# A two-layer decoder trunk on one core: forget-gate sums by matrix products, layer 1's residual gate later in the weight stream, and more pieces open to two engines

## The chip, the cores and the metric

One core of a Trainium2 chip runs the whole kernel in one launch. The metric is the device time of the execution in microseconds (us). The engines are named as the profile names them: PE (TensorE), PEld (its weight loads), DVE (VectorE), ACT (ScalarE), POOL (GpSimd) and SP (the queue that issues the DMAs, SPq in the rows).

## The reference

The input is x with 256 rows and 1,024 columns, in f32. Each of the two layers does the same frame around a different mixer:

```
shift, scale, gate = split(silu(c) @ ada_w[layer] + ada_b[layer], 3)
h = rmsnorm(x, pre_g[layer]) * (1 + scale) + shift
y = mixer(h)                      # even: SSD + block attention; odd: forgetting attention + S5
x = x + gate * rmsnorm(y, post_g[layer])
```

Layer 0's mixer projects h, runs a causal convolution, an SSD recurrence (16 heads, chunks of 128 rows, decay matrices `exp(segsum(dt * a))`) and, at 256 rows, plain causal attention with 16 heads. Its SSD output is multiplied by silu(z) and RMS-normalised over 1,024 columns. Layer 1's mixer runs attention with 24 heads whose scores carry a forget gate, and an S5 state-space branch with 2,048 complex states:

```
F = cumsum(log_sigmoid(f_raw + fgate_b))            # per head, over the 256 rows
s = q @ k.T / 8 + F[query] - F[key];  s = -inf where key > query;  p = softmax(s)
```

F[query] is the same for a whole row of s and cancels in the softmax, so a kernel has to add only F[key].

## The kernel before

All weights pass through the core once, as a stream of units of 128x2,048 f32 (1 MB) that `stream_order` (L42) lays out and that SP loads into three `raw` buffers. A unit of a projection is taken in two halves of 128x1,024. ACT rounds a half to f32r (`whi`), and DVE or POOL subtracts to get the rest (`wlo`); PE then makes three products (high by high, high by low, low by high). There are four `whi` and four `wlo` buffers. Units of kind "mod" and "gate" are not multiplied on PE: DVE reduces a "mod" unit against the condition vector (`modulate`, L822, which makes one column of scale and one of shift), and sums a "gate" unit row by row into `acc` (`ada_piece`, L794: one TENSOR_SCALAR and three SCALAR_TENSOR_TENSOR of 128x512 for the first of two units, four of the latter for the second). `ada_done` (L807) turns `acc` into the product of gate and post-norm weights, `gpt`.

No order of instructions is written by hand. The program records all operations, each for an engine; `Plan.schedule` (L501) orders them by a list scheduler with costs and due times and searches over due times with a fixed seed; `issue` then writes each engine's instructions in the order found. That is why nearly all rows carry line L534. An operation recorded by `either2` (L674) may go to DVE or POOL, as the search decides; one recorded with `G.` goes to POOL, one with `V.` to DVE. A stream order, a buffer count or a cost that changes gives another order everywhere.

The stages follow the stream. Layer 0: the convolution's units and the first "mod" units; z, v and qk units, beside which the SSD is done in four groups of four heads (`ssd`, L1382); then out units. In `ssd` POOL multiplies the rounded and the remaining part of the decay rates (`ahi`, `alo`) by a triangular mask (`keep`) into four `r2` tiles of 128x512 for a group, PE sums them along the rows, ACT takes the exponential. POOL also multiplies the SSD's output by silu(z) (zs) and adds up the squares (ssum). Layer 1: v, u, a small projection for the forget gate, zd, zc, v, then twelve qk units, each followed by the attention of a pair of heads; eight S5 pairs are placed between units by `S5_AT`, "glu" follows the ninth qk unit, and out units end the kernel. Layer 1's four "gate" units lie in the stream behind the last four qk units.

Before, F goes to DRAM once (`fd`), and for each pair of heads `fox_add` (L1584) loads its rows back, spread over 128 partitions, by four DMAs into an `A` buffer; POOL adds the causal mask to it. In `attention` (L1051) PE makes the scores of both heads in two `st` banks of PSUM, DVE adds the prepared tile and takes the row's extreme value (CUSTOM_DVE_ANT_0 `b<-st,A`, for 128 and 256 columns, each with a read of its accumulator), ACT takes the exponentials, PE transposes, and so on. `st` has three banks, and S5 pairs use two of them for as long as DVE works on them in place.

Of the kernel before, what the change touches and what calls it, by code (L numbers as in the profile page):

```python
# [41 lines left out]
def stream_order():  # L42
# [21 lines left out]
    for i in range(12):  # L64
        s.append(("in", 1, "qk", i))
        if i == 8:
            s.append(("glu",))
        if i >= 8:
            s.append(gate1.pop(0))
    s += [("out", 1, i) for i in OUT1_ORDER]  # L70
    return s
# [545 lines left out]
def trunk(ctx, tc, par, s5par, x, w, dtw, fw, postg, gateb, out):  # L617
# [189 lines left out]
    def ada_done(l, c):  # L807
        acc = accs.pop((l, c))
        pb = bank("st")
        gb, pg = tmp("b", [P, 512]), tmp("b", [P, 512])  # L810
        n0 = 512 * c
        S.dma_start(gb, gateb[l:l + 1, n0:n0 + 512].to_broadcast([P, 512]))
        S.dma_start(pg, postg[l:l + 1, n0:n0 + 512].to_broadcast([P, 512]))
        parts = tmp("r2", [P, 512]), tmp("r2", [P, 512])
        split(acc, *parts)
        with plan.together():
            for n, t in enumerate(parts):
                T.matmul(pb, onesr, t, start=(n == 0), stop=(n == 1))
        V.tensor_add(gb, pb, gb)
        G.tensor_mul(gpt[:, n0:n0 + 512], gb, pg)  # L820

    def modulate(l, k, halves):  # L822

        md = tmp("s", [P, 2])
        for n, r in enumerate(halves):
            V.tensor_tensor_reduce(out=r, in0=r, in1=condb, scale=1.0, scalar=0.0, op0=ALU.mult, op1=ALU.add,
                                   accum_out=md[:, n:n + 1])
        c = 16 * l + 2 * k
        V.scalar_tensor_tensor(acol[:, l, k:k + 1], md[:, 0:1], adab1[:, c:c + 1], pc("preg", 8 * l + k, 8 * l + k + 1),
                               op0=ALU.add, op1=ALU.mult)  # L830
        V.tensor_add(bcol[:, l, k:k + 1], md[:, 1:2], pc("adab", c + 1, c + 2))
# [218 lines left out]

    def attention(pair, qk, v, addt, y):  # L1051

        sbs = [bank("st"), bank("st")]
        with plan.together(0.72):
            for b in range(2):
                for j in range(2):
                    h = slice(64 * j, 64 * j + 64)
                    T.matmul(sbs[j][:, BLK[b][0]], qk[h, 0, 128 * b:128 * b + 128], qk[h, 1, 0:128 * b + 128],
                             start=(b == 0), stop=(b == 1), skip_group_check=True)
        pTs = []  # L1060
        for j in range(2):
            p, mn, ad = tmp("b", [P, 384]), tmp("s", [P, 4]), addt(j)
            for c, b in BLK:
                V.tensor_tensor_reduce(out=p[:, c], in0=sbs[j][:, c], in1=ad[:, c], scale=-0.125,
                                       scalar=3.0e38, op0=ALU.add, op1=ALU.min, accum_out=mn[:, b:b + 1])
# [26 lines left out]

    def qkdone(i, vt, addt, y):
        def done(pb):
            qk = tmp("qk", [P, 2, SEQ])
            A.activation(qk, pb, AF.Copy)
            attention(i, qk, vt, addt, y)
        return done
# [276 lines left out]
    def x_decayed(q):  # L1375
        c = slice(512 * q, 512 * q + 512)
        G.tensor_mul(v3(xdt[2][:, c]), v3(xdt[0][:, c]), dtd[:, 8 * q:8 * q + 8, None].to_broadcast([P, 8, 64]))

# [3 lines left out]
    def ssd(hg):  # L1382
        ms, pv = [], {}
        for c in range(2):
            for s, src in (("h", ahi), ("l", alo)):
                t = tmp("r2", [P, 4, P])
                G.tensor_tensor(out=t, in0=src.bitcast(F32)[:, c, 4 * hg:4 * hg + 4, None].to_broadcast([P, 4, P]),
                                in1=keep[:, None, :].to_broadcast([P, 4, P]), op=ALU.mult)
                pv[c, s] = t
# [19 lines left out]
        for pr in range(2):  # L1409
# [3 lines left out]
                                   op0=ALU.mult, op1=ALU.add)  # L1413
            G.tensor_mul(zs(pair), ya, zs(pair))
            if pair == 0:
                A.activation(ssum, zs(pair), AF.Square)
            else:
                sq = tmp("a", [P, SEQ])
                A.activation(sq, zs(pair), AF.Square)
                G.tensor_add(ssum, ssum, sq)  # L1420

# [31 lines left out]

    am2 = amask.rearrange("p b k -> p (b k)")
    for i in range(8):
        proj_cm(qkdone(i, vt, lambda j: am2, zs(8 + i)))
        if i == 0:
# [56 lines left out]
    V.tensor_add(fl, fl, fo[:, 0:16, None].to_broadcast([24, 16, 16]))  # L1514
    fd = scratch([24, SEQ], "fd")
    S.dma_start(fd, flf)

# [65 lines left out]

    def fox_add(i):  # L1584
        fb = tmp("A", [P, 2, 3, P])
        for j in range(2):
            src = fd[2 * i + j:2 * i + j + 1, :]
            S.dma_start(fb[:, j, 0:1, :], src[:, 0:128].to_broadcast([P, 128]))
            S.dma_start(fb[:, j, 1:3, :], src.to_broadcast([P, 256]))
        G.tensor_add(fb, fb, amask[:, None, :, :].to_broadcast([P, 2, 3, P]))  # L1590
        return fb.rearrange("p j b k -> p j (b k)")

    def glu():
# [20 lines left out]
    for i in range(12):  # L1614
        fb = fox_add(i)
        proj_cm(qkdone(i, vt1, lambda j, fb=fb: fb[:, j, :], zc(i)))
        s5_at(14 - NV + i)
# [8 lines left out]
    with tc.manual_schedule():  # L1626
# [11 lines left out]

NA = 12

# [109 lines left out]
```

## Time and profile before

| | us |
|---|---|
| runs of the kernel | 572.38, 577.53, 578.82 (median 577.53) |
| the profiled execution | 581.22 |
| its span, from first to last instruction | 579.4 |

The profiled execution had a mean granted TensorE clock of 0.949 of full speed. Its span is what all rows refer to: times are from the span's start. The 1.8 us between span and execution lie around the instructions.

### The profile page before, as it was taken

How to read it: one execution, taken by the hardware profiler on the slowest of the kernel's cores; microseconds unless marked ns; L12 is line 12 of the kernel's file. 1: busy time of each engine (PE TensorE's matmuls, PEld its weight loads, DVE VectorE, ACT ScalarE, POOL GpSimd, SP SyncE). 2: the span in 40 equal slices, each digit the busy share in tenths (PEclk: the TensorE clock that was granted, in tenths of full speed). 3: DMA queues.
4: the chain of work that ended last, by engine and by line, in shares of the span. 5: the costliest groups of instructions: out<-in, count | busy, mean ns of one | idle time of the engine just before them, and what ended most of it. 6: DMA issues, size and time to landing. Idle time of an engine off the chain costs nothing.

```text
span 579.4 us, 10569 instructions
## 1 busy us (share of the span) xinstructions
PE 529.4 (91%) x3948; PEld 471.7 (81%) x3948; DVE 495.1 (85%) x1084; ACT 367.5 (63%) x759; POOL 121.1 (21%) x107
## 2 busy tenths in 40 slices
PE   7899969899999999896999999999989829999995
PEld 5799969789998897684999997899969617887784
DVE  7998999889989989877669989799998798788764
ACT  5546966564768776356565467367667757789641
POOL 3000315739331000001000222011313434300000
PEclk9999979899999999998799999799989858999998
DMA  8999256376323466993234274054254546635602
GB/s 311 410 408 342 74 181 250 122 258 229 145 95 141 188 245 261 345 353 133 74 111 181 93 283 146 1 218 147 92 206 137 155 157 208 221 125 212 240 24 73
DMA packets 25575, 110.02 MB, mean 190 GB/s; under 512 B 2844, under 2 KB 9652, under 8 KB 15284
## 3 DMA queue, kind: packets, MB, share of 16 engines
q1 hardware_dynamic: 25524, 109.35, 51.6%
q8 instruction: 31, 0.51, 0.3%
q14 instruction: 20, 0.16, 0.1%
HBM read 108.26 MB, written 1.07 MB: 189 GB/s over the span
## 4 chain that ended last, share of the span: by engine, by line
PE 64%; DVE 20%; ACT 6%; DMA 5%; issue 3%; SPq 0%; POOL 0%; POOLq 0%; DVEq 0%; ACTq 0%
PE mm L534 50%; PE st L534 9%; PE y L534 5%; DVE wlo L534 5%; DMA raw<-in_w_dram 4%; DVE b L534 4%; ACT b L534 2%; ACT whi L534 2%; DVE D L534 2%; DVE tb L534 2%; DVE a L534 2%; DVE st L534 1%; DMA A<-in_w_dram 1%; DVE acc L534 1%; DVE raw L534 1%
## 5 line engine op out<-in xcount | busy, mean ns | idle before, releaser
L534 ACT ACTIVATE whi<-raw 128x1024 fp32r<-128x1024 f32 x124 | 128.6, 1053 | 72.9 <-PE mm L534 48.5
L534 DVE TENSOR_TENSOR wlo<-raw,whi 128x1024 fp32r<-128x1024 f32 x112 | 142.1, 1281 | 18.7 <-ACT whi L534 18.1
L534 PE MATMUL mm<-hhi,wlo 128*128 128x256 f32 x656 | 95.8, 289 | 3.9 <-DVE wlo L534 3.9
L534 PE MATMUL mm<-hhi,whi 128*128 128x256 f32 x664 | 95.5, 285 | 2.6 <-ACT whi L534 2.6
L534 PE MATMUL mm<-hlo,whi 128*128 128x256 f32 x664 | 94.5, 283 | 0.0
L534 PEld LDWEIGHTS mm<-hhi,wlo 128*128 128x128 f32 x656 | 85.7, 194 | 8.3 <-DVE wlo L534 4.7
L534 PEld LDWEIGHTS mm<-hhi,whi 128*128 128x128 f32 x664 | 85.6, 191 | 5.5 <-ACT whi L534 3.0
L534 PEld LDWEIGHTS mm<-hlo,whi 128*128 128x128 f32 x664 | 84.7, 190 | 2.5 <-issue 2.4
L534 ACT ACTIVATE b<-b,s 128x256 f32<-128x256 f32 (+1 forms) x160 | 65.9, 445 | 22.4 <-DVE s L534 21.8
L534 PE MATMUL mm<-whi,r 128*128 128x512 f32 x240 | 68.7, 395 | 1.3 <-ACT whi L534 1.3
L534 PEld LDWEIGHTS mm<-whi,r 128*128 128x128 f32 x240 | 44.2, 188 | 11.7 <-ACT whi L534 1.7
L534 POOL TENSOR_TENSOR wlo<-raw,whi 128x1024 fp32r<-128x1024 f32 x12 | 30.3, 2532 | 104.7 <-ACT whi L534 104.7
L534 ACT ACTIVATE b<-tb,s5r 128x256 f32<-128x256 f32 (+3 forms) x128 | 42.2, 385 | 14.4 <-DVE tb L534 13.5
L534 DVE CUSTOM_DVE_ANT_0 raw<-raw,condb 128x1024 f32<-128x1024 f32 x32 | 38.3, 1216 | 1.5 <-DMA raw<-in_w_dram 1.5
L534 PE MATMUL mm<-wlo,r 128*128 128x512 f32 x120 | 38.9, 395 | 0.7 <-DVE wlo L534 0.6
L534 DVE TENSOR_TENSOR tb<-b 128x16 f32<-128x16 f32 (+3 forms) x124 | 30.1, 282 | 7.5 <-ACT b L534 7.0
L534 POOL TENSOR_TENSOR A<-A,amask 128x768 f32<-128x768 f32 x12 | 22.4, 1870 | 54.1 <-DMA A<-fd 47.2
L534 POOL TENSOR_TENSOR s<-s,nhalf 128x1 f32<-128x1 f32 (+1 forms) x9 | 6.0, 675 | 117.8 <-DVE s L534 108.1
L534 PE MATMUL st<-ident,b 128*128 128x128 f32 x128 | 20.6, 284 | 9.5 <-DVE s L534 5.4
L534 PEld LDWEIGHTS mm<-wlo,r 128*128 128x128 f32 x120 | 22.1, 188 | 6.3 <-DVE wlo L534 1.6
L534 PE MATMUL st<-qk 64*128 64x128 f32 (+1 forms) x160 | 21.2, 373 | 5.8 <-DVE b L534 5.8
L534 PEld LDWEIGHTS st<-ident,b 128*128 128x128 f32 x128 | 14.8, 143 | 14.1 <-ACT b L534 12.7
(219 smaller groups left out, 938.1 us busy)
## 6 DMA issues: line engine op xcount, KB each, us to landing
raw<-in_w_dram SPq DMA_DIRECT2D x80, 1024.0 KB, 4.9
raw<-in_w_dram SPq DMA_DIRECT2D x16, 512.0 KB, 10.4
A<-in_w_dram SPq DMA_DIRECT2D x14, 512.0 KB, 10.3
A<-fd SPq DMA_DIRECT2D x24, 128.0 KB, 4.2
A<-fd SPq DMA_DIRECT2D x24, 64.0 KB, 4.7
xres<-in_x_dram SPq DMA_DIRECT2D x2, 512.0 KB, 5.1
b<-in_gateb_dram SPq DMA_DIRECT2D x4, 256.0 KB, 6.0
b<-in_postg_dram SPq DMA_DIRECT2D x4, 256.0 KB, 6.9
```

The source lines that it names most:

```text
L534: getattr(self.engines[e], method)(*[at(v) for v in a], **{n: at(v) for n, v in k.items()})
```

## The change

- Forget gate: `fd`, `fox_add`, its 49 DMAs and 12 POOL additions go. F is kept in SBUF as a rounded part and a rest (`fr`, 2 x 24 rows, the same again in the upper 64 partitions), made by three ACT copies and a DVE subtraction. For each pair of heads PE makes four products of f32r operands ahead of the score products, in the same PSUM banks: a column of `pickf`, repeated 128 times, picks the head's two rows and adds them to all rows of s. DVE then adds the plain mask `amask`, as in layer 0.
- Layer 1's four "gate" units move in the stream from behind qk units 8 to 11 to behind the first four out units.
- `either2` takes the place of `G.` for the decay rows (`r2`), the decayed x, the z products, the sums of squares and `gpt`.
- In layer 1, `modulate` keeps its sums in a tile of 8 x 2 columns and adds bias and scale for four at a time (three operations) where it did two for each.
- `NA` falls from 12 to 11 buffers of 128x1,024, `b` rises from 7 to 8 buffers of 128x512, and `S5_AT` moves pairs 3 to 8 one unit earlier.

```diff
@@ stream_order
         if i == 8:
             s.append(("glu",))
-        if i >= 8:
+    for i in OUT1_ORDER:
+        s.append(("out", 1, i))
+        if gate1:
             s.append(gate1.pop(0))
-    s += [("out", 1, i) for i in OUT1_ORDER]
@@ ada_done, modulate
-        G.tensor_mul(gpt[:, n0:n0 + 512], gb, pg)
+        either2("tensor_mul", gpt[:, n0:n0 + 512], gb, pg)
...
-        md = tmp("s", [P, 2])
+        md = tmp("s", [P, 2]) if l == 0 else md1[:, k, :]
...
+        if l == 1:
+            if k % 4 == 3:
+                ks = slice(k - 3, k + 1)
+                V.tensor_add(bcol[:, 1, ks], md1[:, ks, 1], ab4[:, 1, ks, 1])
+                V.tensor_add(md1[:, ks, 0], md1[:, ks, 0], ab1[:, 1, ks, 0])
+                V.tensor_mul(acol[:, 1, ks], md1[:, ks, 0], pre2[:, 1, ks])
+            return
@@ attention
+        if gates:
+            pick, rows = gates
+            with plan.together(0.3):
+                for b in range(2):
+                    for j in range(2):
+                        h, n = slice(64 * j, 64 * j + 64), 2 * pair + j
+                        T.matmul(sbs[j][:, BLK[b][0]], pick[h, n:n + 1].to_broadcast([64, P]), rows[h, 0:128 * b + 128],
+                                 start=(b == 0), stop=False, skip_group_check=True)
...
-            p, mn, ad = tmp("b", [P, 384]), tmp("s", [P, 4]), addt(j)
+            p, mn = tmp("b", [P, 384]), tmp("s", [P, 4])
             for c, b in BLK:
-                V.tensor_tensor_reduce(out=p[:, c], in0=sbs[j][:, c], in1=ad[:, c], scale=-0.125,
+                V.tensor_tensor_reduce(out=p[:, c], in0=sbs[j][:, c], in1=am2[:, c], scale=-0.125,
@@ x_decayed, ssd
-        G.tensor_mul(v3(xdt[2][:, c]), v3(xdt[0][:, c]), dtd[:, 8 * q:8 * q + 8, None].to_broadcast([P, 8, 64]))
+        either2("tensor_mul", v3(xdt[2][:, c]), v3(xdt[0][:, c]), dtd[:, 8 * q:8 * q + 8, None].to_broadcast([P, 8, 64]))
...
-                G.tensor_tensor(out=t, in0=src.bitcast(F32)[:, c, 4 * hg:4 * hg + 4, None].to_broadcast([P, 4, P]),
-                                in1=keep[:, None, :].to_broadcast([P, 4, P]), op=ALU.mult)
+                either2("tensor_mul", t, src.bitcast(F32)[:, c, 4 * hg:4 * hg + 4, None].to_broadcast([P, 4, P]),
+                        keep[:, None, :].to_broadcast([P, 4, P]))
...
-            G.tensor_mul(zs(pair), ya, zs(pair))
+            either2("tensor_mul", zs(pair), ya, zs(pair))
...
-                G.tensor_add(ssum, ssum, sq)
+                either2("tensor_add", ssum, ssum, sq)
@@ forget gate
-    fd = scratch([24, SEQ], "fd")
-    S.dma_start(fd, flf)
+    G.memset(fr.bitcast(F32), 0.0)
+    i4 = ident.rearrange("p (g n) -> p g n", n=32)
+    V.tensor_add(pickf[0:64], i4[0:64, 0], i4[0:64, 1])
+    V.tensor_add(pickf[64:P], i4[64:P, 2], i4[64:P, 3])
+    A.activation(fr[0:24], flf, AF.Copy)
+    sub2(fr[32:56], flf, fr[0:24].bitcast(F32))
+    for n in range(2):
+        A.activation(fr[64 + 32 * n:88 + 32 * n], fr[32 * n:32 * n + 24].bitcast(F32), AF.Copy)
...
-    def fox_add(i):
-        fb = tmp("A", [P, 2, 3, P])
-        for j in range(2):
-            src = fd[2 * i + j:2 * i + j + 1, :]
-            S.dma_start(fb[:, j, 0:1, :], src[:, 0:128].to_broadcast([P, 128]))
-            S.dma_start(fb[:, j, 1:3, :], src.to_broadcast([P, 256]))
-        G.tensor_add(fb, fb, amask[:, None, :, :].to_broadcast([P, 2, 3, P]))
-        return fb.rearrange("p j b k -> p j (b k)")
@@ constants
-NA = 12
+NA = 11
-S5_AT = (0, 1, 3, 5, 7, 9, 11, 13)
+S5_AT = (0, 1, 2, 4, 6, 8, 10, 12)
-        "D": (2048, 1), "a": (256, 5), "b": (512, 7),
+        "D": (2048, 1), "a": (256, 5), "b": (512, 8),
```

How the scheduler's order comes out is seen in the two programs. Their instructions were counted by kind. PE has 48 more (24 of 128 and 24 of 256 columns, `st<-fr,pickf`). POOL has 17 subtractions `wlo<-raw,whi` of 128x1,024 where it had 12, and 4 of the 16 decay products where it had all; DVE has the other 12, 4 of the 8 z products, 5 of the 7 sums of squares and 2 of the 4 `gpt` products, and 107 subtractions `wlo<-raw,whi` where it had 112. SP has 131 DMA instructions where it had 180.

The first place is POOL and DVE in layer 0, where the SSD's first two groups are prepared (`r` are the `r2` tiles, `dtd` and `cbt` are decay factors). POOL before:

```order
L534 TENSOR_TENSOR alo<-dtk,ahi 128x32
L534 TENSOR_TENSOR r_75<-ahi,keep 128x512
L534 TENSOR_TENSOR r_78<-ahi,keep 128x512
L534 TENSOR_TENSOR r_79<-alo,keep 128x512
L534 TENSOR_TENSOR r_76<-alo,keep 128x512
L534 TENSOR_TENSOR A_113<-A_2_488,dtd 128x512
L534 TENSOR_TENSOR r_77<-alo,keep 128x512
```

and DVE now, where the same products stand between subtractions for the next weights:

```order
L535 TENSOR_TENSOR wlo_72<-raw_63,whi_66 128x1024
L535 TENSOR_TENSOR r_75<-alo,keep 128x512
L535 TENSOR_TENSOR r_76<-alo,keep 128x512
L535 TENSOR_TENSOR wlo_71<-raw_65,whi_68 128x1024
L535 TENSOR_TENSOR r_75<-ahi,keep 128x512
L535 TENSOR_SCALAR acc_74<-raw_64,cond 128x512
```

So the products have moved from a queue of their own into the one that also makes `wlo`.

The second place is DVE in layer 1, at the last S5 pair (`s5mag` is its scan, `s_` with 128x1 the accumulator of a row's extreme value, `A_2_3343` the tile of `fox_add`). Before:

```order
L534 SCALAR_TENSOR_TENSOR b_94<-s5mag,st_128 128x256 x2
L534 RECIPROCAL s_96<-s_96 128x2
L534 SCALAR_TENSOR_TENSOR acc_74<-raw_65,cond,acc_74 128x512
L534 ISA b_92,s_100<-st_127,A_2_3343 128x128
L534 ISA s_100 128x1
L534 ISA b_92,s_100<-st_127,A_2_3343 128x256
L534 ISA s_100 128x1
L534 TENSOR_TENSOR b_93<-b_94,tb_109 128x512
L534 RECIPROCAL s_100<-s_100 128x2
L534 SCALAR_TENSOR_TENSOR acc_74<-raw_65,cond,acc_74 128x512
```

and now:

```order
L535 SCALAR_TENSOR_TENSOR b_90<-s5mag,st_128 128x256 x2
L535 ISA b_96,s_103<-st_126,amask 128x256
L535 ISA s_103 128x1
L535 RECIPROCAL s_103<-s_103 128x2
L535 TENSOR_TENSOR b_93<-b_90,tb_110 128x512
L535 ISA b_94,s_101<-st_128,amask 128x128
L535 ISA s_101 128x1
L535 ISA b_94,s_101<-st_128,amask 128x256
```

The sums into `acc` are gone from here. Of the 24 wide row-extreme instructions of layer 1 (128x256), 17 followed the last S5 scan before, and 19 do now. The first sum into `acc` of layer 1 stood behind 6 of the 24; now it stands behind 14.

The third place is PE where a pair of heads begins (`qk` are its queries and keys), now:

```order
L535 MATMUL mm_125<-hhi,wlo_71 128x256 x8
L535 MATMUL st_126<-fr,pickf 128x128
L535 MATMUL st_127<-fr,pickf 128x128
L535 MATMUL st_126<-fr,pickf 128x256
L535 MATMUL st_127<-fr,pickf 128x256
L535 MATMUL st_126<-qk_82 128x128
L535 MATMUL st_127<-qk_82 128x128
L535 MATMUL st_126<-qk_82 128x256
L535 MATMUL st_127<-qk_82 128x256
L535 MATMUL mm_124<-hhi,whi_67 128x256 x8
```

The gate products stand right ahead of the score products in ten of the twelve pairs; in two, other rows of PE lie between.

## Rows read from the trace of the kernel before

**Rows 1.** The page's head: the span, the engines' busy time, share of the span and instructions, and the chain that ended last by engine.

```profile
span 579.4 us, 10569 instructions
PE 529.4 (91%) x3948; PEld 471.7 (81%) x3948; DVE 495.1 (85%) x1084; ACT 367.5 (63%) x759; POOL 121.1 (21%) x107
...
PE 64%; DVE 20%; ACT 6%; DMA 5%; issue 3%; SPq 0%; POOL 0%; POOLq 0%; DVEq 0%; ACTq 0%
```

**Rows 2.** Busy time by stretch of the span. The columns are the stretch, its length, busy us (and instructions) of PE, PEld, DVE, ACT and POOL, the granted clock, the DMA engines' mean busy share, and GB/s.

```profile
72.00:148.00 76.00, 67.58 (x543) 63.94 (x542) 69.77 (x99) 47.12 (x65) 41.07 (x34) 0.93 0.55 202
148.00:264.00 116.00, 113.85 (x793) 97.60 (x792) 99.72 (x271) 76.52 (x166) 9.45 (x18) 1.00 0.60 226
264.00:284.00 20.00, 14.44 (x74) 12.62 (x73) 17.37 (x45) 13.55 (x37) 2.22 (x4) 0.74 0.30 106
357.00:371.00 14.00, 11.84 (x69) 10.48 (x68) 12.16 (x28) 5.79 (x12) 2.45 (x1) 0.76 0.15 64
457.00:481.00 24.00, 11.59 (x60) 7.42 (x64) 21.66 (x55) 13.88 (x37) 9.13 (x7) 0.54 0.46 152
481.00:510.00 29.00, 28.42 (x246) 23.89 (x239) 21.96 (x63) 22.07 (x64) 11.40 (x6) 0.97 0.64 215
```

**Rows 3.** Who waited for whom from 450 to 510 us: us in total, times, the longest.

```profile
PE st L534 <- DVE b L534: 5.8, 1, 5.8
PE st L534 <- DVE s L534: 5.4, 1, 5.4
PE st L534 <- ACT b L534: 2.6, 4, 0.9
```

**Rows 4.** Single instructions of the timeline from 466 to 480 us: start, length, engine, operation, tiles, shape, and in brackets the idle time before it with what ended it.

```profile
466.68 0.48 DVE L534 TENSOR_SCALAR acc<-raw,cond 128x512 f32<-128x512 f32 x1
470.31 1.65 PE L534 MATMUL st<-qk 64*128 64x128 f32 x6 [5.84 <-DVE b L534]
476.41 0.72 DVE L534 SCALAR_TENSOR_TENSOR acc<-raw,cond,acc 128x512 f32<-128x512 f32 x1
477.37 0.90 PE L534 MATMUL st<-ident,b 128*128 128x128 f32 x3 [5.41 <-DVE s L534]
```

**Rows 5.** The instructions on the tile `acc` alone: DVE's and ACT's busy us in the first and the second of two stretches (then clock, DMA share and GB/s of the stretch).

```profile
457.00:481.00 24.00, 2.88 (x5) 0.00 (x0) 0.54 0.46 152
481.00:510.00 29.00, 3.32 (x5) 0.62 (x1) 0.97 0.64 215
```

**Rows 6.** The timeline of DVE and of POOL at four places, as rows 4.

```profile
87.50 1.04 POOL L534 TENSOR_TENSOR r<-alo,keep 128x512 fp32r<-128x512 f32 x1
87.56 2.06 DVE L534 TENSOR_TENSOR wlo<-raw,whi 128x1024 fp32r<-128x1024 f32 x1
...
90.54 1.21 DVE L534 TENSOR_TENSOR wlo<-raw,whi 128x1024 fp32r<-128x1024 f32 x1
...
359.46 2.45 POOL L534 TENSOR_TENSOR wlo<-raw,whi 128x1024 fp32r<-128x1024 f32 x1 [10.69 <-ACT whi L534]
359.93 2.13 DVE L534 TENSOR_SCALAR a<-a 128x256 f32<-128x256 f32 x1
...
487.36 2.22 POOL L534 TENSOR_TENSOR A<-A,amask 128x768 f32<-128x768 f32 x1 [2.71 <-DMA A<-fd]
488.81 0.41 DVE L534 CUSTOM_DVE_ANT_0 b<-st,A 128x256 f32<-128x256 f32 x1
490.06 1.84 POOL L534 TENSOR_TENSOR A<-A,amask 128x768 f32<-128x768 f32 x1 [0.49 <-DVE s L534]
490.36 1.82 DVE L534 TENSOR_TENSOR a<-a,a 128x256 f32<-128x256 f32 x1
```

**Rows 7.** Groups of instructions by operation, tiles and shape: count, busy us, mean ns of one, idle time before them.

```profile
L534 DVE TENSOR_TENSOR A<-ident,cr 128x512 fp32r<-128x512 f32 x4 | 2.5, 684 | 0.0
L534 DVE TENSOR_TENSOR A<-y,A 128x256 f32<-128x256 f32 x20 | 8.4, 421 | 4.1 <-PE y L534 4.0
L534 POOL TENSOR_TENSOR r<-ahi,keep 128x512 fp32r<-128x512 f32 x8 | 10.4, 1312 | 5.5 <-PE st L534 5.5
L534 POOL TENSOR_TENSOR r<-alo,keep 128x512 fp32r<-128x512 f32 x8 | 10.0, 1252 | 5.1 <-PE st L534 5.0
L534 POOL TENSOR_TENSOR A<-A,amask 128x768 f32<-128x768 f32 x12 | 22.4, 1870 | 54.1 <-DMA A<-fd 47.2 <-DVE acc L534 4.5 <-DVE tb L534 1.8
L534 POOL TENSOR_TENSOR wlo<-raw,whi 128x1024 fp32r<-128x1024 f32 x12 | 30.3, 2532 | 104.7 <-ACT whi L534 104.7
L534 DVE SCALAR_TENSOR_TENSOR acol<-s,adab,pt 128x1 f32<-128x1 f32 x16 | 3.4, 212 | 0.0
L534 DVE TENSOR_TENSOR bcol<-s,pt 128x1 f32<-128x1 f32 x16 | 2.4, 149 | 0.0
```

**Rows 8.** PE and its weight loads around the score products of one pair, in layer 1, as rows 4.

```profile
440.80 1.10 PE L534 MATMUL mm<-hhi,whi 128*128 128x256 f32 x8
441.74 1.09 PE L534 MATMUL mm<-hlo,whi 128*128 128x256 f32 x8
442.76 0.93 PE L534 MATMUL st<-qk 64*128 64x128 f32 x8
443.61 1.00 PEld L534 LDWEIGHTS mm<-hhi,wlo 128*128 128x128 f32 x8 [0.33 <-issue]
```

**Rows 9.** Busy time by stretch as rows 2: layer 0's out units, between which four "mod" units are streamed, and the end of layer 1's out units.

```profile
226.00:264.00 38.00, 35.99 (x160) 28.34 (x159) 29.29 (x43) 17.86 (x21) 0.00 (x0) 1.00 0.90 341
...
547.00:567.00 20.00, 20.00 (x90) 16.54 (x89) 9.88 (x11) 7.41 (x8) 0.00 (x0) 1.00 0.15 53
```

More of the change, by code (lines that the diff above doesn't have):

```diff
@@ L819, in ada_done @@
         V.tensor_add(gb, pb, gb)
-        G.tensor_mul(gpt[:, n0:n0 + 512], gb, pg)
+        either2("tensor_mul", gpt[:, n0:n0 + 512], gb, pg)
+    md1 = const([P, 8, 2], "md1")
+    ab4, ab1 = (t.rearrange("p (l k n) -> p l k n", l=2, n=2) for t in (pc("adab"), adab1))
+    pre2 = pc("preg").rearrange("p (l k) -> p l k", l=2)
     def modulate(l, k, halves):
-        md = tmp("s", [P, 2])
+        md = tmp("s", [P, 2]) if l == 0 else md1[:, k, :]
         for n, r in enumerate(halves):
@@ L1049, in trunk, with attention @@
     BLK = ((slice(0, 128), 0), (slice(128, 384), 1))
-    def attention(pair, qk, v, addt, y):
+    am2 = amask.rearrange("p b k -> p (b k)")
+    def attention(pair, qk, v, y, gates):
         sbs = [bank("st"), bank("st")]
+        if gates:
[6 more added lines that the diff above has]
+                                 start=(b == 0), stop=False, skip_group_check=True)
         with plan.together(0.72):
@@ L1058, in attention @@
                     T.matmul(sbs[j][:, BLK[b][0]], qk[h, 0, 128 * b:128 * b + 128], qk[h, 1, 0:128 * b + 128],
-                             start=(b == 0), stop=(b == 1), skip_group_check=True)
+                             start=(b == 0 and not gates), stop=(b == 1), skip_group_check=True)
         pTs = []
         for j in range(2):
-            p, mn, ad = tmp("b", [P, 384]), tmp("s", [P, 4]), addt(j)
+            p, mn = tmp("b", [P, 384]), tmp("s", [P, 4])
             for c, b in BLK:
-                V.tensor_tensor_reduce(out=p[:, c], in0=sbs[j][:, c], in1=ad[:, c], scale=-0.125,
+                V.tensor_tensor_reduce(out=p[:, c], in0=sbs[j][:, c], in1=am2[:, c], scale=-0.125,
                                        scalar=3.0e38, op0=ALU.add, op1=ALU.min, accum_out=mn[:, b:b + 1])
@@ L1091, in attention, with qkdone @@
         V.tensor_mul(y, yb[:, 0:256], y)
-    def qkdone(i, vt, addt, y):
+    def qkdone(i, vt, y, gates=None):
         def done(pb):
@@ L1096, in done @@
             A.activation(qk, pb, AF.Copy)
-            attention(i, qk, vt, addt, y)
+            attention(i, qk, vt, y, gates)
         return done
@@ L1451, in trunk @@
             f()
-    am2 = amask.rearrange("p b k -> p (b k)")
     for i in range(8):
-        proj_cm(qkdone(i, vt, lambda j: am2, zs(8 + i)))
+        proj_cm(qkdone(i, vt, zs(8 + i)))
         if i == 0:
@@ L1514, in trunk @@
     V.tensor_add(fl, fl, fo[:, 0:16, None].to_broadcast([24, 16, 16]))
-    fd = scratch([24, SEQ], "fd")
-    S.dma_start(fd, flf)
+    fr = const([P, SEQ], "fr", R32)
+    pickf = const([P, 32], "pickf", R32)
+    G.memset(fr.bitcast(F32), 0.0)
[6 more added lines that the diff above has]
+        A.activation(fr[64 + 32 * n:88 + 32 * n], fr[32 * n:32 * n + 24].bitcast(F32), AF.Copy)
     prod = tmp("D", [P, 4, 2, SEQ])
@@ L1614, in trunk @@
     for i in range(12):
-        fb = fox_add(i)
-        proj_cm(qkdone(i, vt1, lambda j, fb=fb: fb[:, j, :], zc(i)))
+        proj_cm(qkdone(i, vt1, zc(i), (pickf, fr)))
         s5_at(14 - NV + i)
```

## The prediction

> **What bounds the kernel now.** I read the page's head first. PE is busy for 91% of the span and is 64% of the chain that ended last; DVE is busy for 85% and is 20% of the chain [rows 1]. So PE's own work sets most of the time, and what else is to be had lies where PE waits. The table by stretch shows where that is [rows 2]. From 148 to 264 us PE is busy for 113.85 of 116 us at full clock. From 457 to 481 us it is busy for 11.59 of 24, at a clock of 0.54: counted at full clock this is about 11.59 x 0.54 = 6.3 us of work, so 17.7 us are lost in this one place. Smaller losses lie at 72 to 148 (8.4 us idle, clock 0.93), at 264 to 284 between the layers, and at 357 to 371.
>
> In the bad stretch DVE is busy for 21.66 of 24 us. That is the engine that decides there, though its share of the whole span is below PE's. The waits say how [rows 3]: PE waited once for 5.8 us for DVE's `b` and once for 5.4 us for DVE's `s`. The timeline places them [rows 4]: the score products at 470.31 wait for a bank that the last S5 pair still holds, the transposes at 477.37 for a softmax, and DVE meanwhile sums into `acc`.
>
> A third reading concerns DVE and POOL together. A subtraction `wlo` takes 1.21 us on DVE, but 2.06 where POOL began a product at 87.50; a TENSOR_SCALAR that waits beside POOL's `wlo` at 359.46 takes 2.13; a 128x256 product beside POOL's addition at 490.06 takes 1.82, where the like of it takes 0.42 [rows 6, 7]. Each time DVE's instruction ends when, or just after, POOL's has ended and DVE has done its own work. The CUSTOM_DVE instruction at 488.81, which reads PSUM, takes 0.41 beside POOL's addition: it is not held. So POOL's work is not free: it adds 0.8 to 1.9 us to a DVE instruction that reads or writes SBUF alone.
>
> The Trainium skill says so too (GPSIMD Engine Reference, 1. Specifications): POOL shares its SBUF interfaces with VectorE and contends with instructions that have two SBUF inputs or use both ports. The rows at 490.06 and 488.81 agree; by the rule alone moving a product from POOL to DVE costs less than DVE's time for it, which is the lower end of term 2.
>
> **The change part by part.** The sum starts from the profiled execution, 581.2 us (span 579.4 and 1.8 around it), which is 3.7 above the median of the runs, 577.5. I work out a difference and take it from the median.
>
> Term 1, the late attention. Layer 1's sums into `acc` leave this place: 2.88 us of DVE in 457 to 481 and 3.32 in 481 to 510 [rows 5]. The order shows none beside the last S5 pair, and the first behind 14 wide row-extremes where it was behind 6. The twelve POOL additions go as well (1.87 us each); at least the one at 490.06 held DVE for 1.4 us, and I put two or three such holds, 1 us each, into these 53 us. And the last S5 pair is done ahead of 19 of 24 wide row-extremes where it was 17, so it meets fewer softmaxes. In the 24 us, DVE's 21.66 fall by 2.88 and about 1.5, to 17.3 us, against 6.3 of PE's work: 4.4 us are saved where DVE runs without a gap. More comes when PE has more to do meanwhile and keeps its clock: the half clock costs 11.59 - 6.3 = 5.3 us there. I take 4.4 + 5.3 = 9.7, so -10. The ends are 0 (the S5 pair still holds the banks) and -17.7 (the whole loss).
>
> Term 2, layer 0's products. DVE gets 12 decay products at 0.62 to 0.69 (the 128x512 product with repeated operands takes 684 ns), 4 z products and 5 sums at 0.42, 2 `gpt` products at 0.68: 8.2 + 3.8 + 1.4 = 13.4 us. It loses 5 subtractions `wlo` at 1.21, 6.1 us, to POOL. Alone this is +7.3 us of DVE work. Against it stand the holds: some 23 POOL instructions vanish there that each held DVE by up to 0.85 us [rows 6], so up to 19.5 us; five new POOL `wlo` hold it by up to 1.9, 9.5 us. By these, DVE's net lies between +7.3 + 9.5 and +7.3 - 19.5, the middle is near 1. DVE is busy 69.77 of 76 us, and 99.72 of 116, in the two stretches [rows 2], so some of it shows at PE in the first and hardly any in the second. A product also reaches PE 0.6 us sooner (1.25 to 1.31 on POOL). I take -2, with ends +7 and -7.
>
> Term 3, the gate products. 48 PE instructions are new. Ordinary f32r products of 256 columns follow each other by 0.94 / 8 = 0.117 us [rows 8]; eight instructions of the score products take 0.93 in all, also 0.117 each, for 128 and 256 columns mixed. At that rate a pair's four cost 0.47, twelve pairs 5.6 us. If two heads' products run side by side in the array's halves, they take half, 2.8. No row shows a weight that is one column repeated; loading it could be late by some 0.2 for each, but a loss beyond 7 would need that for every one. Going back to full-array weights shows 0.33 us of idle [rows 8]; the order puts gate and score products side by side in ten pairs, so only two pay it again. Some of it falls in waits for `qk`. I take +3.5, ends +2 and +7.
>
> The Trainium skill (TensorEngine Tiling (Array Packing), Key Properties) says that a change of tiling mode drains the engine. The 0.33 us agree; by the rule twelve separate switches would make 4 us more, but the order leaves two.
>
> Term 4, layer 1's out units. Half of the `acc` work (and its raw units) comes between them. Layer 0 has the same pattern, four units reduced by DVE between out units, and PE is idle there for 2.0 of 38 us at 341 GB/s, while layer 1's clean end shows 20.00 of 20 [rows 9]. I take +1.5, ends 0 and +5.
>
> Term 5, the rest. 49 DMAs leave the SP queue in which weights wait too; the other POOL additions stop holding DVE; layer 1's columns are 16 + 16 small instructions of which half go (8 x 0.21 + 8 x 0.15 = 2.9 us, against 6 new ones of 0.15). Three ACT copies and some small DVE instructions for `fr` come, beside POOL's memset, before the first pair needs them. I take -2, ends 0 and -4.
>
> The sum is -10 - 2 + 3.5 + 1.5 - 2 = -9, so 572.2 by the profiled execution and 568.5 by the median.
>
> **The rivals.** The wait stays: the last S5 pair holds two of three `st` banks as before, and the gate products, now first in those banks, wait in PE's queue as the score products did. For it: 5.8 us of the loss were that wait [rows 3]. Against it: DVE comes to the pair's steps sooner with `acc` gone. Then term 1 is -1 and the change is 0, so 577.5.
>
> The whole loss goes: PE has work ready, its clock stays up, term 1 is -17.7, and half of the holds' lower end in term 2 comes: -17 to -19 in all, so 559. For it: DVE has 4.4 us less to do and the S5 pair meets fewer softmaxes. Against it: POOL's five more `wlo` hold DVE for up to 1.9 us each.
>
> It gets slower: DVE becomes the bound in layer 0, from 72 to 264 us. There it gets 13.4 us of products and gives 6.1 away. Free DVE time is 6.2 us in the first 76 and 16.3 in the next 116; once `wlo` comes later than PE asks for it, each us is a us. If the holds do not shrink, that is +7.3, with +7 for gate products whose weights are loaded late and term 1 at -5: +7.3 + 7 - 5 + 1.5 - 2 = +9, so 586. It decides from the point where DVE's share in 148 to 264 passes 95%.
>
> **How the numbers follow.** Forecast 0.46 (own range 563 to 574), whole loss 0.20, wait stays 0.22, slower 0.12. About 1% is what a measurement of this kernel tells from no change: below 571.8 or above 583.3. Faster: 0.20 + 0.85 of 0.46 + a little of 0.22 = 0.60; slower: nearly all of the last case, 0.11; the rest, 0.29, is the same. The range leaves out half of the slowest case and a part of the fastest: 557 to 581.
>
> **What would show it.** Right, step by step: no stretch of 20 us near the last S5 pair with PE under 60% and a clock near 0.5; no `acc` sums there; DVE instructions of 1.8 to 2.3 us gone where `r<-alo` and `A<-A,amask` ran; `st<-fr,pickf` within 0.5 us for a pair and no new idle before it; layer 1's out units with PE above 94%. Wrong: PE waiting for DVE at `st<-fr,pickf` by 5 us or more, PE below 95% from 148 to 264 us with DVE above 95%, or gate products of over 0.6 us a pair.

## The result and the profile after

The changed kernel takes 557.93 us in the median of 4 runs (557.44 to 558.36); the kernel before takes 577.70 beside it (572.38 to 578.82). The ratio is 0.9675 with a 95% interval of 0.9615 to 0.9735, so it is faster by 19.8 us. The forecast was 9 us less, 568.5. Medians here are over all runs; the ratios leave disturbed runs out, so the two need not agree to the last tenth.

The page's head of the changed kernel's profile, and its chain by engine:

```profile
span 556.1 us, 10554 instructions
PE 521.6 (94%) x3996; PEld 467.7 (84%) x3996; DVE 480.5 (86%) x1077; ACT 366.9 (66%) x761; POOL 99.2 (18%) x97
...
PE 68%; DVE 17%; ACT 8%; issue 4%; DMA 1%; SPq 0%; POOLq 0%; POOL 0%; DVEq 0%; ACTq 0%
```

Against [rows 1] the span is 23.3 us shorter; 3.5 of them are the spread of the kernel before, whose profiled execution took 581.22 us against the median of 577.70. PE is busy for 7.8 us less although it has 48 more instructions; its mean granted clock is 0.974 where it was 0.949. DVE is busy for 14.6 us less.

Busy time by stretch, columns as in [rows 2]. The first three stretches are layer 0's two and the one between the layers; the next four follow PE's products of the projections, whose output is `mm` (the 1,345th, 1,985th, 2,369th and 2,625th of 2,896, then the end). First the kernel before, in its stretches of layer 1, then the changed one:

```profile
284.00:374.20 90.20, 88.04 (x716) 83.31 (x715) 74.18 (x148) 50.70 (x96) 11.66 (x7) 0.96 0.37 131
374.20:435.10 60.90, 57.73 (x497) 52.05 (x495) 58.62 (x133) 40.90 (x96) 12.72 (x6) 0.97 0.44 161
435.10:504.20 69.10, 54.63 (x422) 44.87 (x421) 57.80 (x156) 48.21 (x128) 26.78 (x15) 0.83 0.52 170
504.20:579.00 74.80, 68.20 (x397) 54.48 (x395) 51.65 (x114) 45.18 (x106) 5.62 (x5) 0.97 0.40 141
```

```profile
72.00:146.00 74.00, 69.15 (x575) 65.93 (x574) 72.58 (x113) 46.68 (x68) 17.72 (x16) 0.98 0.57 201
146.00:260.50 114.50, 113.07 (x793) 97.11 (x792) 98.36 (x267) 78.09 (x170) 15.12 (x16) 1.00 0.60 227
260.50:280.00 19.50, 12.64 (x78) 11.32 (x77) 17.32 (x44) 14.28 (x40) 5.99 (x7) 0.82 0.31 118
280.00:363.50 83.50, 83.40 (x711) 79.89 (x711) 70.90 (x148) 51.61 (x99) 8.16 (x4) 1.00 0.38 140
363.50:416.50 53.00, 53.00 (x475) 49.34 (x474) 52.10 (x118) 37.40 (x84) 17.05 (x11) 1.00 0.47 167
416.50:479.70 63.20, 56.62 (x466) 46.81 (x465) 50.17 (x150) 50.71 (x140) 14.97 (x16) 0.92 0.26 95
479.70:556.00 76.30, 69.91 (x422) 56.25 (x421) 56.14 (x122) 44.43 (x103) 1.10 (x2) 0.99 0.46 166
```

These rows show where the 23 us went. Layer 0 gives 4. The first 136 us of layer 1, up to 416 us, give 14.6: PE is now busy without a gap there, and its clock stays at 1.00. Only 6 come in the stretch with the last S5 pair, the one place that the forecast's largest term was about. The end takes 1 us more. A new order can also move work from one of these stretches to the next, as the table in 4 shows.

Who waited for whom in that stretch (416 to 480 us), and PE's timeline where the two long waits of [rows 3, 4] have become 2.77 and 2.72 us:

```profile
PE st L535 <- DVE b L535: 2.8, 1, 2.8
PE st L535 <- ACT b L535: 2.7, 1, 2.7
PE mm L535 <- ACT qk L535: 1.0, 2, 0.7
```

```profile
442.58 0.32 PE L535 MATMUL st<-fr,pickf 64*128 64x128 f32 x1
445.67 0.79 PE L535 MATMUL st<-fr,pickf 64*128 64x128 f32 x3 [2.77 <-DVE b L535]
446.06 1.69 PE L535 MATMUL st<-qk 64*128 64x128 f32 x8
450.46 1.09 PE L535 MATMUL st<-ident,b 128*128 128x128 f32 x3 [2.72 <-ACT b L535]
```

The instructions on `acc` alone, as [rows 5]: none stand beside the last S5 pair.

```profile
440.00:469.30 29.30, 0.00 (x0) 0.00 (x0) 0.83 0.10 37
469.30:490.50 21.20, 2.72 (x4) 0.00 (x0) 1.00 0.33 113
```

Groups that answer to [rows 7]: the decay products on both engines, `wlo` on POOL, and the gate products with their weight loads.

```profile
L535 DVE TENSOR_TENSOR r<-ahi,keep 128x512 fp32r<-128x512 f32 x5 | 3.2, 682 | 0.0
L535 DVE TENSOR_TENSOR r<-alo,keep 128x512 fp32r<-128x512 f32 x7 | 4.6, 680 | 0.0
L535 POOL TENSOR_TENSOR r<-ahi,keep 128x512 fp32r<-128x512 f32 x3 | 3.3, 1098 | 21.1 <-ACT ahi L535 21.1
L535 POOL TENSOR_TENSOR wlo<-raw,whi 128x1024 fp32r<-128x1024 f32 x17 | 41.6, 2455 | 102.9 <-ACT whi L535 97.1 <-DVE A L535 4.1 <-PE mm L535 1.6
L535 PE MATMUL st<-fr,pickf 64*128 64x128 f32 x24 | 5.3, 341 | 2.8 <-DVE b L535 2.8
L535 PEld LDWEIGHTS st<-fr,pickf 64*128 64x128 f32 x48 | 4.8, 200 | 5.2 <-DVE b L535 3.2 <-issue 1.2 <-DVE s L535 0.2
```

The products cost DVE 0.68 us each, as forecast. The holds of [rows 6] became fewer. I take each DVE instruction that overlaps one of POOL and is longer than the lower quartile of its form by over 0.2 us, and add up the excess: some 39 instructions with 33 us before, some 25 with 20 after (29 to 36 and 17 to 21 us by other ways of forming the groups). No DVE instruction without POOL beside it has such an excess. The twelve additions into `A` held some 7 DVE instructions for some 6.5 us; they are gone.

Layer 1's out units answer to [rows 9], with their `acc` sums between them; PE is busy for 99%:

```profile
490.50:550.00 59.50, 59.10 (x329) 46.35 (x327) 45.07 (x96) 35.48 (x82) 0.55 (x1) 1.00 0.50 181
```

### The profile page after: what moved, and what is told of

Its sections match the earlier page's. It is cut to its first block, busy times and chain, and to the rows that moved or that the text cites. A ratio compares the mean times of both kernels' runs of the same rounds, so it can differ in the third digit from the quotient of the medians.

```text
span 556.1 us, 10554 instructions
## 1 busy us (share of the span) xinstructions
PE 521.6 (94%) x3996; PEld 467.7 (84%) x3996; DVE 480.5 (86%) x1077; ACT 366.9 (66%) x761; POOL 99.2 (18%) x97
## 4 chain that ended last, share of the span: by engine, by line
PE 68%; DVE 17%; ACT 8%; issue 4%; DMA 1%; SPq 0%; POOLq 0%; POOL 0%; DVEq 0%; ACTq 0%
PE mm L535 52%; PE st L535 11%; PE y L535 5%; DVE b L535 5%; DVE wlo L535 4%; ACT whi L535 3%; DVE st L535 2%; ACT b L535 2%; DVE a L535 2%; DMA A<-in_w_dram 1%; DVE tb L535 1%; ACT A L535 1%; ACT L535 1%; ACT a L535 1%; DVE acc L535 1%
## 5 line engine op out<-in xcount | busy, mean ns | idle before, releaser
L535 DVE TENSOR_TENSOR wlo<-raw,whi 128x1024 fp32r<-128x1024 f32 x107 | 132.1, 1246 | 21.1 <-ACT whi L535 20.8
L535 PE MATMUL mm<-hhi,wlo 128*128 128x256 f32 x656 | 93.0, 282 | 0.0
L535 PEld LDWEIGHTS mm<-hhi,wlo 128*128 128x128 f32 x656 | 83.0, 188 | 3.3 <-issue 3.1
L535 ACT ACTIVATE b<-b,s 128x128 f32<-128x128 f32 (+1 forms) x160 | 65.8, 446 | 18.6 <-DVE s L535 18.2
L535 POOL TENSOR_TENSOR wlo<-raw,whi 128x1024 fp32r<-128x1024 f32 x17 | 41.6, 2455 | 102.9 <-ACT whi L535 97.1
L535 ACT ACTIVATE b<-tb,s5r 128x64 f32<-128x64 f32 (+3 forms) x128 | 41.0, 383 | 7.2 <-DVE tb L535 5.0
L535 DVE CUSTOM_DVE_ANT_0 b<-st,amask 128x128 f32<-128x128 f32 (+1 forms) x80 | 24.1, 351 | 1.6 <-PE st L535 1.4
L535 DVE TENSOR_TENSOR tb<-b 128x16 f32<-128x16 f32 (+3 forms) x110 | 19.9, 219 | 4.3 <-ACT b L535 3.8
L535 PE MATMUL mm<-wlo,hhi 128*128 128x256 f32 x144 | 23.2, 283 | 0.1
L535 PE MATMUL mm<-whi,hhi 128*128 128x256 f32 x144 | 23.0, 281 | 0.0
```

Source lines behind the costliest of these rows:

```text
L535: getattr(self.engines[e], method)(*[at(v) for v in a], **{n: at(v) for n, v in k.items()})
```

## The experiments

Each kernel is one edit of the kernel before (B) or of the changed one (A). In most the planner orders everything anew. In four (called fixed order) all operations are recorded and ordered as in their parent, and some are then not issued. Runs of B beside them had medians of 579 to 582 us, so ratios to B are given.

**1. What another order alone is worth.** The seed of the search was changed in both kernels.

```diff
-SEED = 2
+SEED = 3
```

B: 

> The kernel before with another seed of the planner's search (3 in place of 2) and nothing else. Theory P (the parts of the change carry the time): within 4 us of the kernel before, 573 to 582. Theory S (the order that the search happens to find carries it): more than 6 us away from it, on either side, and the long waits of PE in layer 1 stand in other places.

A: 

> The changed kernel with another seed of the planner's search (3 in place of 2) and nothing else. Theory P (the parts of the change carry the time): 554 to 562. Theory S (the order that the search found for the changed kernel happened to be good): 564 or more.

Measured: B 577.41, ratio 0.9952 (0.9914 to 0.9989). A 562.99, 5.1 above the changed kernel, ratio 0.9710 (0.9657 to 0.9764). By the totals theory P holds for B, and A lies between the two theories. So reordering alone moves 2.9 us in B and 5.1 in A (2.0 by A's two ratios), and the change is worth 14 us with seed 3 and 20 with seed 2. One more seed was tried, not many. Inside layer 1 the order moved far more than that, as the table in 4 shows.

**2. The parts alone, in B.** The products of the gate with the new buffers; the gate units' place; `either2`; `S5_AT`.

```diff
# b_gate_units
-        if i >= 8:
-            s.append(gate1.pop(0))
...
+        if gate1:
+            s.append(gate1.pop(0))
# b_either (and the like in four more places)
-            G.tensor_mul(zs(pair), ya, zs(pair))
+            either2("tensor_mul", zs(pair), ya, zs(pair))
# b_s5
-S5_AT = (0, 1, 3, 5, 7, 9, 11, 13)
+S5_AT = (0, 1, 2, 4, 6, 8, 10, 12)
```

Products: 

> The kernel before with the forget gate's part of the change alone (gate products, plain mask, 11 buffers of 128x1,024 and 8 of 128x512). Theory P: the additions on POOL and their tiles were what made DVE late in layer 1, so 567, with the waits at 357 to 371 and at 416 to 436 gone. Rival of the forecast's own terms: +3.5 for the products and -1.5 for what goes, so 579. Theory S: anything between 570 and 584, by other places than those two.

Gate units: 

> The kernel before with layer 1's four gate units moved between the out units and nothing else. Theory P as the forecast had it (late attention -10, out units +1.5): 569. Rival, the last S5 pair sets the wait and not the sums: 577 to 579. Theory S: anything between 570 and 584.

`either2`: 

> The kernel before with the decay rows, z products, sums of squares and gpt open to DVE and nothing else. Theory P: 573.5, all of it in layer 0 (4.4 us were gained there by the whole change). Rival, DVE becomes the bound: 584 with PE under 95% from 148 to 264 us. Theory S: a change of more than 4 us in layer 1, where nothing but gpt was opened.

`S5_AT`: 

> The kernel before with S5_AT of the changed kernel (pairs 3 to 8 one unit earlier) and nothing else. Theory L (the last S5 pair came too late before; one unit earlier it is out of the way of the score products): about 10 us less than before, 568 to 570, and no stretch with the clock near 0.5 between 440 and 500 us. Rival (the room that the other parts make is needed for it): within 4 us of before.

Measured: products 568.25, 0.9792 (0.9744 to 0.9839); gate units 571.26, 0.9832 (0.9783 to 0.9880); `either2` 574.63, 0.9884 (0.9825 to 0.9944); `S5_AT` 578.55, 0.9934 (0.9880 to 0.9987). Products, gate units and `either2` come within 2.3 us of theory P's numbers, the gate units for a reason that 4 does not bear out; but `either2` also moved layer 1 by more than 4 us (table in 4), as theory S had it. `S5_AT` alone gives hardly more than another seed; theory L falls. The four together would be 5.6%, against 3.3% for the whole; each also contains a new order, which by 1 is worth some 0.5% in B.

**3. The parts taken out of A.** The same edits backwards; with the old forget gate go 12 buffers of 128x1,024 and 7 of `b`.

Gate units: 

> The changed kernel with layer 1's four gate units at their old place (behind qk units 8 to 11) and nothing else. The forecast's terms 1 and 4 with the sums' own price as measured at a fixed order (3 us or less): 556 to 561. If the sums make the order of the late attention bad, as term 1 had it: 566 to 569.

Forget gate: 

> The changed kernel with the old forget gate (the DRAM round trip, POOL's twelve additions, 12 buffers of 128x1,024 and 7 of 128x512) and nothing else. By the prices at a fixed order (2 us saved for the products, 2 us more for the additions): 556 to 561. If the additions, their tiles and their waits make the order bad: 566 to 570.

`S5_AT`: 

> The changed kernel with the old S5_AT and nothing else. Theory L: the long waits at the last S5 pair come back, 566 to 570. Rival (the other parts carry it): 556 to 562.

`either2`: 

> The changed kernel with the decay rows, decayed x, z products, sums of squares and gpt back on POOL alone. By the run of that part alone (6.7 us less than before): 563 to 567. Rival, DVE is the bound of layer 0 in the changed kernel and is helped: 556 or less.

Measured: 566.59, 572.50, 563.37 and 563.81, which is 8.7, 14.6, 5.4 and 5.9 above the changed kernel. Against A with the other seed (562.99) they are 3.6, 9.5, 0.4 and 0.8 above. Against the changed kernel by ratios they are 5.7, 12.0, 2.3 and 4.0 us. So the forget gate's part is the largest from either side, and out of A it came out above both of its expected ranges. The gate units come next; their 566.6 is the number expected if they spoil the order, not the one for the sums' own price. The other two are not told apart from a new order by their totals: `S5_AT` lies between its two ranges, `either2` in the first of its own.

**4. One price at a time, at a fixed order.** Not issued were POOL's twelve additions, 14 of 16 sums into `acc`, and half of the last S5 pair's DVE work, all in B; and the 48 gate products in A.

```diff
# b_no_mask_adds: left out
-        G.tensor_add(fb, fb, amask[:, None, :, :].to_broadcast([P, 2, 3, P]))
# b_no_acc: left out where l == 1
-                V.scalar_tensor_tensor(acc, r[:, k, :], wk, acc, op0=ALU.mult, op1=ALU.add)
# b_light_s5: left out where i0 == 14
-            V.tensor_mul(ts, pb, sin)
-            V.tensor_mul(pb, pb, cos)
-            V.tensor_add(pb[:, 0, :], pb[:, 0, :], ts[:, 1, :])
-            V.tensor_sub(pb[:, 1, :], pb[:, 1, :], ts[:, 0, :])
# a_no_products: left out
-                        T.matmul(sbs[j][:, BLK[b][0]], pick[h, n:n + 1].to_broadcast([64, P]), rows[h, 0:128 * b + 128],
-                                 start=(b == 0), stop=False, skip_group_check=True)
```

Additions: 

> The kernel before in its own order, instruction for instruction, but POOL's twelve additions of the mask in layer 1 are not issued (the scores then lack the causal mask). Theory H (the additions make DVE late, by holding its instructions and by handing over the tile late): the 6 to 7 us of DVE time that they cost beside 8 of its instructions come back where DVE is late, so 4 to 7 us less than before. Theory O (where each step stands in DVE's queue sets the waits): less than 1.5 us.

Sums: 

> The kernel before in its own order, but 14 of layer 1's 16 sums into acc are not issued (its gate is then that of the first quarter alone). Term 1 of the forecast, taken by itself: the two waits of 5.8 and 5.4 us at 470 and 477 us shrink, 4.4 to 10 us less than before. Theory O: those waits stand on the last S5 pair and on the softmax, not on the sums, so less than 3 us.

S5 work: 

> The kernel before in its own order, but of the last S5 pair eight DVE instructions (both halves' rotation into the scan) are not issued, some 4.4 us of DVE work (the last two S5 channels then lack the rotation). Theory O (the wait of 5.8 us at 470 stands on the S5 pair's place in DVE's queue): 3.5 to 6 us less than before. Rival (PE would wait for the softmax instead): under 1.5 us.

Products: 

> The changed kernel in its own order, but the 48 gate products are not issued (the scores then lack the gate). Term 3 of the forecast: 3.5 us less than the changed kernel, so 554.5 (bounds 2 and 7). Rival, products are hidden in waits for qk: under 1 us less, 557 to 558.

Measured: additions 0.9971 (0.9912 to 1.0030), sums 0.9942 (0.9896 to 0.9988), S5 work 1.0028 (0.9964 to 1.0091); products 556.08 (554.95 to 557.29), 1.9 us less than the changed kernel (4.6 by the two ratios, 0.9595 and 0.9675, of different hours). So by their ratios the three in B are worth 1.7 us, 3.4 us and nothing, and their intervals reach to 5.1, 6.0 and 2.1 us less. The products cost 2 to 5 us. PE's waits from 450 to 512 us without the sums, then without the S5 work:

```profile
PE st L537 <- ACT b L537: 8.0, 5, 5.4
PE st L537 <- DVE b L537: 5.9, 1, 5.9
```

```profile
PE st L537 <- DVE b L537: 4.6, 1, 4.6
PE st L537 <- DVE s L537: 3.6, 1, 3.6
```

Without the sums the two waits stand as in [rows 3], 5.9 and 5.4 us (the second now put down to ACT): the sums were not what PE waited for. Without half of the S5 work the waits shrink by 1.2 and 1.8, so that work stands ahead of them; yet the whole is no faster, and theory O's 3.5 to 6 us did not come. By their times the sums and the additions lie between the two theories' ranges. For the sums the waits decide for theory O; for the additions they stand too (6.1 and 5.4 us), but the interval leaves room for theory H's lower end of 4 us.

Where the orders differ was then read by the progress of PE. For each profile the table gives the us from the start to the 1,345th `mm` product (layer 0), the three steps to the 1,985th, 2,369th and 2,625th (layer 1's mixer) with their sum, and the rest:

```
kernel         layer 0   step 1  step 2  step 3 | sum     rest   span
before          284.1     90.1    60.9    69.1  | 220.1   75.2   579.4
b_seed3         284.9     84.4    52.0    80.9  | 217.3   72.6   574.9
b_s5            284.2     89.5    71.8    55.0  | 216.3   76.3   576.8
b_either        279.3     86.6    68.5    73.1  | 228.2   69.7   577.1
b_gate_units    286.7     84.4    80.2    44.5  | 209.1   73.9   569.6
b_products      289.1     83.8    53.4    68.0  | 205.2   73.1   567.4
after           280.1     83.4    53.0    63.3  | 199.7   76.4   556.1
a_seed3         281.7     83.6    53.0    65.3  | 201.9   76.1   559.7
a_gateold       282.6     83.5    53.0    68.6  | 205.1   76.2   563.9
a_s5old         283.8     83.9    53.2    69.1  | 206.2   73.6   563.6
a_pool          284.3     83.4    53.0    63.9  | 200.3   76.2   560.7
a_fox           286.8     88.9    57.6    61.6  | 208.1   75.0   569.9
```

These are single profiles of single orders. The three fixed-order kernels of B have B's order, and their layer 0 took 284.6 to 287.1 us, their sums 215.6 to 218.8: differences of 3 us in layer 0 and of 4 in the sum can be another execution alone. There is a pattern all the same. All orders here with the gate by products (and its new buffers) have steps 1 and 2 of 83 to 84 and 53 us. Those with the old gate spread over 52 to 80 in step 2 and give in step 3 what they took in 2, or the other way round: the sum stays at 208 to 228. With `either2` alone layer 0 takes 4.8 us less, and 4.2 more without it; but kernels with layer 0's operations as in their parent move it as much (5.0 more in `b_products`, 3.7 more in `a_s5old`), so that this is `either2` and not the order is not shown.

**5. The eighth buffer.** The forget gate's part also brings 8 `b` buffers instead of 7 (for one of 128x1,024 less). Softmax, S5 and its tables all take them.

```diff
# a_b7, in A
-"b": (512, 8)
+"b": (512, 7)
# b_b8, in B
-NA = 12
+NA = 11
-"b": (512, 7)
+"b": (512, 8)
# a_na10_b10, in A
-NA = 11
+NA = 10
-"b": (512, 8)
+"b": (512, 10)
```

A with seven: 

> The changed kernel with 7 buffers of 128x512 for b in place of 8 and nothing else (still 11 of 128x1,024). Theory B (the eighth b buffer is what the forget gate's part brings: softmax and S5 pair compete for b): 566 to 572, with most of the 12 to 15 us of that part lost. Theory G (the additions, their tiles and POOL's port bring it): 556 to 562.

B with eight: 

> The kernel before with 8 buffers for b and 11 of 128x1,024 and nothing else (the additions of the gate stay). Theory B: 567 to 572. Theory G: 576 to 584, one A buffer less being a loss if anything.

A with ten: 

> The changed kernel with 10 buffers for b in place of 8 and 10 of 128x1,024 in place of 11, the same memory, and nothing else. Theory B: faster again, 550 to 556, if the A buffer isn't missed. Rival (eight are enough, and the A buffer is missed): 558 to 565.

Measured: A with seven 571.46, which is 13.5 above the changed kernel (11.2 by the two ratios, 0.9869 and 0.9675); B with eight 571.67, ratio 0.9880 (0.9800 to 0.9960), some 7 us below B (2 to 12 by the interval); A with ten 560.74, 2.8 above the changed kernel. The first two lie in theory B's ranges, the third in the rival's: ten, with one buffer of 128x1,024 less, brought nothing. In A the two kernels with seven took 571.5 and 572.5, the six with eight or more 557.9 to 566.6, whatever else differs. In B the six that were ordered with seven took 571.3 to 582, the two with eight 568.3 and 571.7. So the number of buffers counts in A beyond a new order; in B its size is not told well from the 0.5% of another seed. Each of these kernels also shares the work out anew: A with seven gives POOL 81 instructions where the changed kernel gives it 97, and DVE is busy for 493.7 us instead of 480.5. With the old gate instead of the products (`a_fox`) A takes 572.50, with seven buffers alone 571.46: no more of that part than the buffer can be told in A. In B the products with the buffer have 0.9792, the buffer alone 0.9880, and the intervals touch. Layer 1's three steps with eight in B, then with seven in A:

```profile
284.00:367.40 83.40, 83.08 (x714) 79.76 (x713) 72.09 (x145) 50.02 (x94) 11.80 (x6) 1.00 0.40 149
367.40:423.30 55.90, 55.37 (x486) 50.84 (x487) 55.41 (x132) 41.07 (x93) 15.55 (x7) 1.00 0.46 161
423.30:493.00 69.70, 53.23 (x431) 44.20 (x429) 61.35 (x159) 44.21 (x126) 25.53 (x18) 0.85 0.47 152
```

```profile
285.70:377.10 91.40, 85.58 (x713) 82.03 (x713) 80.10 (x173) 55.74 (x110) 5.73 (x3) 0.96 0.38 137
377.10:449.30 72.20, 64.56 (x535) 57.07 (x535) 67.98 (x165) 50.16 (x121) 12.10 (x9) 0.95 0.30 108
449.30:494.00 44.70, 44.70 (x406) 39.75 (x405) 37.62 (x104) 33.62 (x83) 2.69 (x1) 1.00 0.42 150
```

The first two steps take 139 us in B with eight and 164 in A with seven, but the third gives this back: the sums are 209.0 and 208.3. Each has to be compared with its own parent. With the eighth buffer B's sum falls from 220.1 to 209.0 and its layer 0 stays (284.0). Without it A's sum rises from 199.7 to 208.3 and its layer 0 from 280.1 to 285.7.

**6. Who lacks it.** In B, the S5 tables' first three steps take their work tile from the `a` buffers.

```diff
-            x = tmp("b", [P, 2, 2, 128])[:, :, :, 0:m]
+            x = (tmp("a", [P, 2, 2, m]) if m < 128 else tmp("b", [P, 2, 2, 128]))
```

> The kernel before, with the same buffers, but the S5 table's first three doubling steps of four (of 16, 32 and 64 columns) take their work tile from the five buffers of 128x256 that are little used in layer 1 (a), not from the seven of 128x512 (b); only the last step still takes a b. Theory B, form 1 (the tables are what lacks b): 566 to 572, and the S5 banks wait less for DVE than the 217 us of the kernel before. Theory B, form 2 (what counts is a b left free for the softmax while an S5 quad holds its four products): within 4 us of the kernel before.

Measured: 576.67, ratio 0.9965 (0.9923 to 1.0007). The S5 banks did wait less for DVE: 172 us, added over 16 channels from the first S5 product into a bank to DVE's first instruction on it, where B has 217 and the changed kernel 169. But the time is B's: steps 1 and 2 are 81.7 and 53.8 us, and step 3 is 79.0. Form 1 falls. Form 2 agrees with the number, but was not tried by itself.

## Why the prediction was wrong

The sign and the kind of loss were right: PE had waited for DVE in layer 1, and now it waits less. The size was half of what was measured: 9 us were forecast, and 10.8 more came.

**The rest (term 5) is the step that failed.** It priced instructions and DMAs and put -2. The line that takes `b` from 7 to 8 stands in the account of the change and had no term at all. Taking the eighth buffer out of A costs 11 to 13.5 us, and giving it to B saves some 7, with 2 to 12 left open; that is of the size that was missing. The waits did not show it: of the 161 times that a `b` buffer is taken anew after 300 us in the kernel before, 4 come within 0.6 us of its last use, and the median is 5.7 us later (worked out from the program's buffer names and the trace). The shortage acts when the order is made: the planner places a step behind the release of its buffer, and in the run the step merely stands late in its engine's queue. That the number of buffers carries time is shown in A, where all orders with seven took longer than all with eight or more. How much of the 19.8 us it carries stays open, since orders, shares of the engines and the other parts move together; the way of acting is argued from the code and those distances.

**Late attention (term 1).** Forecast -10 in 457 to 510 us, by sums into `acc` and holds. Measured are -5.8 in step 3. The waits of 5.8 and 5.4 us halved, but not for want of the sums: with these not issued both waits stand, and the whole loses 0.6%. That DVE is busy for 21.66 of 24 us [rows 2] was read as "less work, shorter wait". The prediction had both causes right, the bank and the softmax, and still counted the sums as part of the waits. Rows of DVE that it did not show speak against that:

```profile
469.00 1.25 DVE L534 TENSOR_TENSOR_SCAN b<-s5mag,st 128x256 f32<-128x256 f32 x2
474.30 0.41 DVE L534 CUSTOM_DVE_ANT_0 b<-st,A 128x256 f32<-128x256 f32 x1
475.18 1.25 DVE L534 TENSOR_TENSOR_SCAN b<-s5mag,st 128x256 f32<-128x256 f32 x2
476.35 0.13 DVE L534 RECIPROCAL s<-s 128x2 f32<-128x2 f32 x1
```

The score products at 470.31 start when the S5 pair's scans of 469.00 have left their bank. The transposes at 477.37 stand behind a softmax whose row extreme comes at 474.30 and whose reciprocal comes at 476.35, right behind the pair's last scans. From the start of the first wait to that reciprocal DVE sums into `acc` once, for 0.48 us at 466.68; the sum at 476.41 [rows 4] comes after it. The S5 pair's steps stand where the order puts them. The gate units' move gives 3.6 to 9.7 us all the same; whether through a new order, or because their raw units no longer lie between the qk units, was not tried.

**Layer 0's products (term 2).** Forecast -2, measured -4.0 in the whole change, -4.8 with this part alone and +4.2 without it; by the table in 4 and the run with seven buffers, other parts move layer 0 as much, so the cause is open. The reason given, fewer of POOL's instructions that hold DVE, agrees with the holds counted above, but was not tried by itself. The bounds that the term works out for DVE (+16.8 and -12.2) have their middle at 2.3, not near 1.

**Gate products (term 3).** Forecast +3.5, measured +1.9 by the medians, just under the lower end, and +4.6 by the two ratios. In eight of the twelve pairs the four take 0.49 or 0.50 us, as worked out. In the pairs at 422, 451 and 457 us they take 0.69 to 1.04, and at 442.58 the wait of 2.77 falls between them; over 0.6 was named as a sign of being wrong. The feared late weight load did not come.

**Out units (term 4).** Forecast +1.5, measured +1.2 in the rest of the span; with the gate units at their old place it is the same 76.2 us, so, as far as two single profiles tell, the units cost nothing there.

**The rivals.** "The whole loss goes" had 559, and 557.9 was measured; but it put all of it at the last S5 pair, while 14.6 of the 23.3 us came before. That its number came true is luck. The wait that stays and the slower case did not come: from 146 to 260 us PE is busy for 99%, DVE for 86%.

## What to carry to other kernels

Where a planner or scheduler makes the order, count what it allocates: here one buffer was worth more in the changed kernel than any work taken out at a fixed order, and the waits in the trace did not say so. Before putting a price on work beside a wait, look whether it stands ahead of the instruction that ends the wait, and take it out at a fixed order. Compare a change of a few per cent with another seed of the search first, since a new order alone moved 2 to 5 us here.

## What was not expected of the hardware

The kernel before spreads over 570.8 to 584.5 us in all runs taken beside these kernels, with a granted clock of 0.944 to 0.970 over its span; the changed kernel stays within 557.4 to 558.4 at 0.974 to 0.979 in its four runs. The long gaps of PE, in one of which the clock was 0.54 [rows 2], have become fewer in it; that they cause the spread was not tried.

The weight loads of the gate products, one column repeated 128 times, took 200 ns in the mean (the row above), with a median of 185, where an ordinary 128x128 tile took 188 in the mean.
